# Accumulator banks handed out by the planner, and a planner that tries more orders

## The chip, the core and the metric

The kernel runs on one core of a Trainium2 chip. The core has five engines that run side by side, each through a list of instructions in a fixed order: TensorE (PE in the profile, with its weight loads shown as PEld), VectorE (DVE), ScalarE (ACT), GpSimd (POOL) and SyncE (SP), which issues most DMA transfers. TensorE writes its products into PSUM, eight banks of 128 x 512 numbers, and VectorE or ScalarE reads them from there. The metric is the device time of one execution in microseconds (us); lower is better.

## What is computed

Two layers of a decoder trunk, for 528 positions (16 learned ones and 512 of the input) of width 1024:

```python
for l in range(DEPTH):                       # 2 layers
    xn = rmsnorm(h, norm_mix_g[l])
    z_ret, z_hgrn, z_rwkv, z_s5 = split_cols(xn @ w_in[l], ...)   # 3360 columns
    o_ret  = retention_mixer(z_ret, pos)     # chunkwise retention
    o_hgrn = hgrn2_mixer(z_hgrn, ...)        # gated linear recurrence
    o_rwkv, v_first = rwkv7_mixer(z_rwkv, v_first, ...)   # generalised delta rule
    o_s5   = s5_mixer(z_s5, ...)             # diagonal complex recurrence
    h = h + concat([o_ret, o_hgrn, o_rwkv, o_s5]) @ w_out[l]
    hn = rmsnorm(h, norm_ffn_g[l])
    h = h + square(relu(hn @ w_ffn_up[l])) @ w_ffn_down[l]
return rmsnorm(h, norm_f_g)[:, N_META:]
```

The four mixers of a layer are independent of each other. They need the projections `xn @ w_in`, and the output projection needs all four.

## The kernel before

**Work.** Activations lie with the features across the partitions and the positions along the free dimension. A large product is done in three passes, since each operand is split into a high and a low part: high times high, high times low, low times high. So one tile of a large product is 24 matmuls (8 blocks of 128 input features, three passes) into one bank. Their outputs are called `pi` (input projection), `po` (output projection), `pu` and `pd` (the two halves of the MLP); the number behind `pi_` or `po_` counts weights and so tells how far the layer is. In layer 0 and in both input projections a matmul has 272 or 256 columns; in the rest of layer 1 it has 512. These four kinds are called weight products below. In all there are 7872 of them: 1296 for each input projection, and the first of the second layer stands behind 4752 others.

**Mixers.** Each mixer works through its positions in three segments, named c0, c3, c6 for RWKV (`L0c0` is layer 0, first segment) and c0, c1, c2 for HGRN (`h`) and retention (`r`: `r1c2` is retention in layer 1, last segment). S5 works in two halves. They are chains of small products: a product into a bank, an operation on VectorE or ScalarE that reads it, the next product. In RWKV the products `G..` open a segment's main part, `pak`, `px` to `pt` solve a triangular system, `S`, `zp` and `po00` to `po12` advance the state and make the output, and `pg0`, `pg1` are the last products of a segment. In retention `rs00` to `rs13` are the eight score products of a segment, each read by one VectorE operation that writes `ATr`; `bkr` is the last product of a segment.

**Order.** Nothing is issued as it is written. `Sched.record` collects the operations. `Sched.flush` plans them, three times in the program: up to the middle of the first layer's MLP, from there to the middle of the second layer's, and the rest. `Sched.run` goes through the operations by list scheduling, with a cost for each operation (`price`) and a latency between engines (`lat`): each engine takes, of the operations that are ready, the one with the lowest key. The key is how late an operation may start, taken from a backward run. `attempt` repeats forward and backward runs (ten times, `TURNS`), and the shortest plan is issued, engine by engine in the planned order. Matmuls with another tile shape (such as 64 x 64) are put off for a while to avoid changing the shape (`KEEP`, `SWITCH`).

**Banks.** Before the change `NPS=[3,3,1,1]` splits the eight banks: three for the weight products (`hv`), three for RWKV (`rw`), one for HGRN (`hg`), and one (`mx`) for retention, S5 and the sums of the norms. Within its share, a product uses the banks in turn, in the order in which the program is written, and must wait until the product that had the bank before is read.

**Fill.** While TensorE would be idle, `run` counts fill matmuls on zeros (operand `zero`, line L236) for that gap. `keep_warm` then puts them into a bank of the weight products that is about to be opened, and leaves them out where there is none.

The change is in `Sched` (`tile`, `run`, `flush`, `keep_warm`) and in `ps`, which the mixers call for a bank. All instructions have line L233, since a helper issues them, so they are told apart by their tiles.

Of the kernel before, what the change touches and what calls it, by code (L numbers as in the profile page):

```python
# [49 lines left out]
STEP=1; WARM=6500.0; LEAST=3500.0; SWITCH=.1; DRAIN=.05; KEEP=3.0; WCOLS=256; WCOST=.112; WSAFE=.4; FLB=2; NPRE=3; TURNS=10; NPS=[3,3,1,1]  # L50
# [8 lines left out]
class _Op:  # L59
    __slots__=("e","op","f","a","k","deps","pre","cost","succ","ready","cols","nbytes","chain","label","pri","order","mode","at")  # L60

TICK=10.24/3
# [25 lines left out]
class Sched:  # L88


    def __init__(s,tc):
        s.tc=tc; nc=s.nc=tc.nc
        s.clk={n:.57 for n in ("tensor","vector","scalar","gpsimd","sync")}; s.queue=(.57,0.0); s.recent=[]; s.tiling=(None,None); s.bank={}; s.tag={}; s.idle=None
# [5 lines left out]
    def tile(s,pool,pn,shape,dt,name,tag,bufs,psum=False):  # L99
        x=pool.tile(shape,dt,name=name,tag=tag,bufs=bufs)  # L100
        n=x.tensor.name
        if psum: s.psum.add(n); s.bank[n]=x; s.tag[n]=tag
        s.tags.setdefault((pn,tag),(bufs,[]))[1].append(n)
        return x
# [30 lines left out]
    def run(s,key,back=False):  # L135
# [3 lines left out]
        clk={e:0.0 for e in s.clk} if back else dict(s.clk); hw,dma=(0.0,0.0) if back else s.queue; mode,place=s.tiling; recent=collections.deque(s.recent); act=sum(x for _,x in recent); idle=[0]*N  # L139
        ready={e:[] for e in clk}; late={e:[] for e in clk}  # L140
        left=[len(o.succ if back else o.pre) for o in ops]; at=[0.0 if back else o.ready for o in ops]; T=[0.0]*N; Z=[0.0]*N
        push=heapq.heappush; pop=heapq.heappop
        for i,o in enumerate(ops):
            if not left[i]: push(late[o.e],(at[i],i))
        for _ in ops:
            t=1e18
            for x in clk:
                p=late[x]; r=ready[x]
                while p and p[0][0]<=clk[x]:
                    i=pop(p)[1]; push(r,(key[i],i))  # L150
                u=clk[x] if r else p[0][0] if p else 1e18
                if u<t: t=u; e=x
            p=late[e]; r=ready[e]
            while p and p[0][0]<=t:
                i=pop(p)[1]; push(r,(key[i],i))
            if e!="tensor" or back: i=pop(r)[1]; o=ops[i]; c=o.cost
            else:


                x=r[0]  # L160
                if ops[x[1]].mode!=mode:
                    y=min((y for y in r if y[0]<x[0]+KEEP and ops[y[1]].mode==mode),default=None)
                    if y is not None: x=y
                o=ops[x[1]]
                if o.at is not None and o.mode==mode and o.at==place:
                    y=min((y for y in r if y[0]<x[0]+KEEP and ops[y[1]].mode==mode and ops[y[1]].at!=place),default=None)
                    if y is not None: x=y
                if x is r[0]: pop(r)
                else: r.remove(x); heapq.heapify(r)
                i=x[1]; o=ops[i]; c=o.cost  # L170

                if o.mode!=mode: c+=SWITCH+(DRAIN if place is not None else 0.0)


                if s.idle is not None:
                    p=clk[e]; n=0; w=WCOLS*max(o.mode[0],64)/128.0; d=WCOST if o.at is None else WCOST/2+.002
                    while n<32:
                        while recent and recent[0][0]<p-TICK: act-=recent.popleft()[1]
                        if p+d<=t:
                            if act<WARM: recent.append((p,w)); act+=w; n+=1  # L180
                            p+=d
                            continue
                        while recent and recent[0][0]<t-TICK: act-=recent.popleft()[1]
                        if act>=LEAST: break
                        recent.append((t,w)); act+=w; n+=1; t+=d; p=t
                    idle[i]=n
# [10 lines left out]
            Z[i]=z  # L197
            for j,l in (o.pre if back else o.succ):
# [3 lines left out]
        return T,Z,(clk,(hw,dma),(mode,place),list(recent),idle)  # L202
    def flush(s,turns=0):
# [4 lines left out]
        for (pn,tag),(bufs,names) in s.tags.items():  # L208
            for q,t in enumerate(names):
# [4 lines left out]
                for i in s.users[t]:  # L214
                    if not ops[i].deps&mine: ops[i].deps|=old; ops[i].ready=max(ops[i].ready,at)
        for o in ops: o.pre=[(j,lat(ops[j],o)) for j in o.deps]+[(j,-1e9) for j in o.order]
# [3 lines left out]
        best=None; key=list(range(len(ops)))  # L220
        def attempt(key,n):
            nonlocal best
            for it in range(n):
                if it: key=chain([-z for z in s.run([-z for z in Z],True)[1]])
                T,Z,state=s.run(key); m=max(Z)
                if best is None or m<max(best[1]): best=T,Z,state
# [3 lines left out]
        T,Z,(s.clk,s.queue,s.tiling,s.recent,idle)=best  # L230
        for t in s.users: s.done[t]=max(Z[i] for i in s.users[t])
        for k,i in s.keep_warm(T,idle):
            if k is None: o=ops[i]; e=o.e; x=o.f(*o.a,**o.k)  # L233
            else:
                K,M,p,q=i; e="tensor"
                x=s.nc.tensor.matmul(s.bank[k][q:q+M,:WCOLS],s.idle[p:p+K,:M],s.idle[p:p+K,:WCOLS],start=True,stop=True)  # L236
            if e in s.prev: s.tc.add_manual_dep(x.ins,s.prev[e].ins.name,mybir.DependencyInfo(mybir.DependencyClass.NoSync,mybir.DependencyReason.DATA),reason="order")
            s.prev[e]=x
        s.start()
    def keep_warm(s,T,idle):  # L240


        ops=s.ops; order=sorted((t,i) for i,t in enumerate(T))
        first={}
        for t,i in order:
            o=ops[i]
            if o.e=="tensor":
                n=(o.k["out"] if "out" in o.k else o.a[0]).tensor.name
                if n not in first: first[n]=t
        bufs,names=next(x for (pn,tag),x in s.tags.items() if tag=="hv" and x[1][0] in s.psum)  # L250
        banks=[]
        for q,n in enumerate(names):
            if n in first: banks.append((first[n],0.0 if q<bufs else s.done.get(names[q-bufs],0.0),n,q%bufs))
        banks.sort()
        out=[]; at=0
        for t,i in order:
            if idle[i]:
                while at<len(banks) and banks[at][0]<t: at+=1
                K,M=[max(x,64) for x in ops[i].mode]; d=WCOST if K==M==128 else WCOST/2+.002; p=t-d*idle[i]
                x=banks[at:at+bufs]; x=x[:1] if K==128 else [y for y in x if y[3]==0][:1]+[y for y in x if y[3]==1][:1]  # L260
                if K==64 and len(x)<2: x=[]
                for j in range(idle[i]):
                    if x:
                        _,f,n,_=x[j%len(x)]
                        if f+WSAFE<=p: out.append((n,(K,M,K*(j%len(x)),M*(j//len(x)%(128//M)))))
                    p+=d
            out.append((None,i))
        return out
# [3 lines left out]
def lat(p,c):  # L272
    if p.nbytes: return .92
    if p.e=="tensor" and c.e=="tensor": return 0.0
    return AFTER[p.e]+(.104 if p.e==c.e=="vector" else .092 if p.e==c.e=="scalar" else WAIT[c.e])
def price(o,out,ins,n):
# [882 lines left out]
def build(tc,A,o_ap):  # L1159
# [4 lines left out]
    with tc.tile_pool(name="kp",bufs=1) as kp, tc.tile_pool(name="ps",bufs=1,space=bass.MemoryType.PSUM) as pp:  # L1164
        np_=[0]; nps=dict(zip(("hv","rw","hg","mx"),NPS))
        def ps(shape,nm,tag):
            t=nc.tile(pp,'ps',[128,512],F32,nm,tag,nps[tag],True)
# [439 lines left out]
```

## Time and profile before

| | |
|---|---|
| median of 3 runs | 1575.28 us (1572.36 to 1577.1) |
| the profiled execution: its time | 1566.77 us |
| the profiled execution: span from the first to the last instruction | 1565.0 us |
| mean granted TensorE clock | 0.969 of full speed |
| TensorE busy | 1510.2 us (96%), of it 75.61 us with fill |
| VectorE busy | 928.6 us (59%) |
| ScalarE busy | 585.2 us (37%) |
| GpSimd busy | 422.3 us (30472 instructions on all engines together) |

An execution's time is 1.8 us above its span. A busy TensorE isn't a useful one: fill counts as busy, and a matmul's time in the profile reaches from its start to its end, so that several overlap. How many weight products start in a stretch says more than the busy share.

### The profile page before, as it was taken

The page shows a single profiled execution, that of the slowest core. Times are in us where ns is not written, and L with a number is a line of the kernel's source. Part 1 is how long each engine was busy: PE and PEld are TensorE (multiplying, and loading weights), DVE is VectorE, ACT ScalarE, POOL GpSimd, SP SyncE. Part 2 cuts the span into 40 slices and gives each one's busy share as a digit, 9 for nine tenths or more (in the row PEclk, how much of TensorE's full clock was granted, in tenths as well). Part 3 has the DMA queues.
Part 4 walks back from the last instruction along what each step waited for, and adds up shares of the span by engine and source line. Part 5 has one row for each costly group of instructions (what it writes and reads, how often), then busy time and mean ns, then how long its engine had stood idle before and what let it go on. Part 6 is the DMA issues. An engine that isn't in the chain of part 4 may idle for free.

```text
span 1565.0 us, 30472 instructions
## 1 busy us (share of the span) xinstructions
PE 1510.2 (96%) x11645; PEld 1362.3 (87%) x11645; DVE 928.6 (59%) x2237; ACT 585.2 (37%) x1163; POOL 422.3 (27%) x577
## 2 busy tenths in 40 slices
PE   8999998989999999999999999989999999999997
PEld 7998887778999999999999998876778888888887
DVE  8855897867843337433565357978757333333345
ACT  4334443522442433424433235445225424233342
POOL 3411572413233225332000012232210222222210
PEclk9999999879999999999999999999889999999998
DMA  5545143421323224332346553352302233332332
GB/s 177 168 130 155 55 125 107 113 72 32 95 87 96 90 77 148 102 96 88 118 150 219 156 156 98 106 154 70 95 28 94 95 95 96 96 98 95 95 103 79
DMA packets 143298, 168.54 MB, mean 108 GB/s; under 512 B 52144, under 2 KB 77168, under 8 KB 143152
## 3 DMA queue, kind: packets, MB, share of 16 engines
q1 hardware_dynamic: 143152, 166.59, 35.1%
q8 instruction: 92, 1.51, 0.4%
q14 instruction: 54, 0.44, 0.1%
HBM read 138.65 MB, written 27.56 MB: 106 GB/s over the span
## 4 chain that ended last, share of the span: by engine, by line
PE 83%; DVE 8%; DMA 2%; issue 2%; SPq 2%; POOL 1%; ACT 1%; DVEq 0%; POOLq 0%; ACTq 0%
PE pu L233 23%; PE pd L233 23%; PE pi L233 17%; PE po L233 6%; SPq L233 2%; PE po L236 1%; DVE Irs L233 1%; DMA Em_L1c<-sd 1%; PE s5y2s L233 0%; DMA X_L0c<-sa 0%; PE s5y0s L233 0%; PE pi L236 0%; DVE Jis L233 0%; PE s5g L233 0%; DVE hA L233 0%
## 5 line engine op out<-in xcount | busy, mean ns | idle before, releaser
L233 ACT ACTIVATE wh<-wr 128x512 fp32r<-128x512 f32 (+1 forms) x388 | 243.8, 629 | 537.2 <-PE pd L233 216.2
L233 DVE TENSOR_TENSOR wl<-wr,wh 128x512 fp32r<-128x512 f32 (+1 forms) x388 | 269.6, 695 | 292.5 <-ACT wh L233 287.4
L233 PE MATMUL pi<-xha,wh 128*128 128x256 f32 (+2 forms) x864 | 252.3, 293 | 5.1 <-ACT zs L233 4.1
L233 PE MATMUL pi<-xla,wh 128*128 128x256 f32 (+2 forms) x864 | 250.3, 290 | 1.0 <-DVE xla L233 1.0
L233 PE MATMUL pi<-xha,wl 128*128 128x256 f32 (+2 forms) x864 | 249.8, 290 | 0.0
L233 PE MATMUL pu<-xhf,wh 128*128 128x272 f32 (+2 forms) x768 | 247.0, 322 | 0.0
L233 PE MATMUL pu<-xhf,wl 128*128 128x272 f32 (+2 forms) x768 | 246.7, 321 | 0.0
L233 PE MATMUL pu<-xlf,wh 128*128 128x272 f32 (+2 forms) x768 | 245.5, 320 | 0.0
L233 PE MATMUL pd<-xhh,wh 128*128 128x256 f32 (+2 forms) x736 | 234.6, 319 | 0.0
L233 PE MATMUL pd<-xhh,wl 128*128 128x256 f32 (+2 forms) x736 | 234.1, 318 | 0.0
L233 PE MATMUL pd<-xlh,wh 128*128 128x256 f32 (+2 forms) x736 | 233.0, 317 | 0.0
L233 POOL TENSOR_TENSOR xlh<-fs,xhh 128x272 fp32r<-128x272 f32 (+1 forms) x96 | 92.2, 961 | 298.6 <-DVE fs L233 230.4
L233 PEld LDWEIGHTS pi<-xha,wh 128*128 128x128 f32 (+1 forms) x864 | 161.8, 188 | 9.1 <-ACT zs L233 4.3
L233 PEld LDWEIGHTS pi<-xla,wh 128*128 128x128 f32 (+1 forms) x864 | 162.1, 188 | 3.7 <-DVE xla L233 1.6
L233 PEld LDWEIGHTS pi<-xha,wl 128*128 128x128 f32 (+1 forms) x864 | 162.1, 188 | 1.7 <-issue 0.5
L233 PEld LDWEIGHTS pu<-xlf,wh 128*128 128x128 f32 x768 | 144.6, 188 | 11.3
L233 PEld LDWEIGHTS pu<-xhf,wl 128*128 128x128 f32 x768 | 144.5, 188 | 11.2
L233 PEld LDWEIGHTS pu<-xhf,wh 128*128 128x128 f32 x768 | 144.4, 188 | 10.6
L233 PEld LDWEIGHTS pd<-xlh,wh 128*128 128x128 f32 x736 | 138.5, 188 | 10.0
L233 PEld LDWEIGHTS pd<-xhh,wl 128*128 128x128 f32 x736 | 138.5, 188 | 9.9
L233 PEld LDWEIGHTS pd<-xhh,wh 128*128 128x128 f32 x736 | 138.6, 188 | 9.4
L233 POOL TENSOR_TENSOR h<-h,fd 128x272 f32<-128x272 f32 (+1 forms) x72 | 87.7, 1218 | 183.2 <-DVE fd L233 181.1
(923 smaller groups left out, 2593.1 us busy)
## 6 DMA issues: line engine op xcount, KB each, us to landing
wr<-in_wup SPq DMA_DIRECT2D x128, 256.0 KB
wr<-in_wdn SPq DMA_DIRECT2D x128, 256.0 KB
wr<-in_win SPq DMA_DIRECT2D x104, 256.0 KB
wr<-in_wout SPq DMA_DIRECT2D x32, 256.0 KB
h<-in_x SPq DMA_DIRECT2D x16, 264.0 KB
hD<-h SPq DMA_DIRECT2D x8, 264.0 KB
h<-hD SPq DMA_DIRECT2D x8, 264.0 KB
out<-out SPq DMA_DIRECT2D x8, 256.0 KB
```

The lines of the kernel that those rows point to most:

```text
L233: if k is None: o=ops[i]; e=o.e; x=o.f(*o.a,**o.k)
L236: x=s.nc.tensor.matmul(s.bank[k][q:q+M,:WCOLS],s.idle[p:p+K,:M],s.idle[p:p+K,:WCOLS],start=True,stop=True)
```

## The change

Banks are no longer split. `ps` now asks `Sched.bank` for a name, not for a bank. `CLASS` puts all four users into one class `a`. While `run` plans, a product's first matmul (`opens`) may start only when a bank is free (`can`). It then takes the bank that came free first. Three banks are set aside for the product that is next in the order of the program (`OWN`, `queue_`, `line`); the other five go to whichever product is most urgent. The bank is free again when its last reader in the plan has ended. Fill is planned at the same place, in banks that are free by then, and `keep_warm` is gone. After the ten turns, `flush` makes 30 more tries (`SHAKES`): each starts from the best keys so far, adds a random number with a spread of 1.0 to each, runs three rounds, and keeps the result when the plan is shorter.

```diff
-STEP=1; ...; TURNS=10; NPS=[3,3,1,1]
+STEP=1; ...; TURNS=10; SHAKES=30; SHAKE=1.0; BANKS=8; CLASS=dict(hv='a',rw='a',hg='a',mx='a'); OWN=dict(a=3)
...
+    def bank(s,pool,name,tag):
+        s.pool=pool; n=f"{name}_v{len(s.psum)}"; s.psum.add(n); s.tag[n]=tag
+        return bass.AP(bass.PSumTensorHandle(name=n,shape=[128,512],dtype=F32),0,[[512,128],[1,512]])
...
+        def can(i,t):
+            v=ops[i].opens
+            if v is None: return True
+            if not free or free[0][0]>t: return False
+            c=s.tag[v]; q=s.queue_[c]
+            while line[c]<len(q) and q[line[c]] in place_: line[c]+=1
+            if q[line[c]]==v and own[c]<OWN[c]: return True
+            return extra<spare
...
+                r_=[y for y in r if can(y[1],t)]
+                if not r_: look=t; continue
...
-                x=r[0]
+                x=min(r_)
...
+                if o.opens is not None:
+                    x=min((y for y in free if y[0]<=t and not (o.mode[0]<128 and y[1] in dirty)),default=None) or free[0]
+                    free.remove(x); heapq.heapify(free); v=o.opens; b=x[1]; k=s.tag[v]
+                    if s.queue_[k][line[k]]==v and own[k]<OWN[k]: own[k]+=1
+                    else: extra+=1; k=None
+                    place_[v]=(b,k)
...
+                for v in o.banks:
+                    use[v]-=1; b,k=place_[v]
+                    s.until[v]=max(s.until.get(v,0.0) if use[v]+1<s.count[v] else 0.0,z+(lat(o,PE_) if e!="tensor" else 0.0))
+                    if not use[v]: push(due,(s.until[v],b,k))
...
+            rnd=random.Random(1)
+            for _ in range(SHAKES):
+                m=max(best[1]); key=[x+rnd.gauss(0.0,SHAKE) for x in keys[0]]; attempt(chain(key),3)
...
-    def keep_warm(s,T,idle):
...
-            t=nc.tile(pp,'ps',[128,512],F32,nm,tag,nps[tag],True)
+            t=nc.bank(pp,nm,CLASS[tag])
```

The instructions themselves stay the same but for fill: 1818 mixer and norm matmuls and 7872 weight products in both programs, with 411 fill matmuls before and 462 now. What moves is their order.

On TensorE, in the first layer, this is where RWKV's first segment opens its main part (`G00L0c`), between input projections `pi`. Before:

```order
L233 MATMUL pi_28_128_272_277<-xha_84,wh_263 128x256
L233 MATMUL pi_28_128_272_277<-xla_85,wh_263 128x256
L233 MATMUL pi_28_128_272_277<-xha_84,wl_264 128x256
L233 MATMUL pi_28_128_272_277<-xha_86,wh_263 128x256
L233 MATMUL pi_28_128_272_277<-xla_87,wh_263 128x256
L233 MATMUL G00L0c_468<-rav_L0c_463,bk_L0c_464 128x128 x2
L233 MATMUL G10L0c_469<-rav_L0c_463,bk_L0c_464 128x128
```

And now, with `b` ahead of a bank's name and `v` behind it:

```order
L304 MATMUL bpi_20_128_0_v_2155<-xha_82,wh_206 128x272
L304 MATMUL bpi_20_128_0_v_2155<-xla_83,wh_206 128x272
L304 MATMUL bpi_20_128_0_v_2155<-xha_82,wl_207 128x272
L304 MATMUL bG00L0c_v_2165<-rav_L0c_398,bk_L0c_399 128x128 x2
L304 MATMUL bG10L0c_v_2170<-rav_L0c_398,bk_L0c_399 128x128
```

It stood in projection 28 and stands in projection 20. Counted through the program, 697 of the layer's 1296 input-projection matmuls stand ahead of it before, and 486 now. For the third segment these are 1296 and 988. In the second layer the first segment moves from 937 to 499, the third from 1296 to 960. HGRN and retention go the other way: HGRN's first product of the first layer (`lv1h0c0`) stood behind 936 and now stands behind 1200.

On TensorE, in the second layer, these are retention's score products of the second segment. Before, with products of HGRN (`lv64`, `tmkh`) and RWKV (`tp`) and a weight product between them:

```order
L233 MATMUL rs01r1c_9332<-rqz1c_9323,rkz1c_9325 128x128
L233 MATMUL lv64h1c_9246<-hB_9184,Kh1c_9233 64x128 x3
L233 MATMUL rs11r1c_9333<-rqz1c_9323,rkz1c_9325 128x128
L233 MATMUL rs02r1c_9334<-rqz1c_9323,rkz1c_9325 128x128
L233 MATMUL po_6_2_16_9396<-xho_9305,wh_8907 128x512
L233 MATMUL rs12r1c_9335<-rqz1c_9323,rkz1c_9325 128x128
L233 MATMUL tp01L1c_9131<-cst,rav_L1c_9109 128x128 x3
L233 MATMUL tp11L1c_9132<-cst,rav_L1c_9109 128x128 x3
L233 MATMUL rs03r1c_9336<-rqz1c_9323,rkz1c_9325 128x128
L233 MATMUL tmkh1c_9248<-cst,Kh1c_9233 128x128
```

And now:

```order
L304 MATMUL brs00r1c_v_15128<-rqz1c_9078,rkz1c_9080 128x128
L304 MATMUL brs11r1c_v_15131<-rqz1c_9078,rkz1c_9080 128x128
L304 MATMUL brs02r1c_v_15133<-rqz1c_9078,rkz1c_9080 128x128
L304 MATMUL bzp2L1c_v_15093<-tav_L1c_8959,tbk_L1c_8960 64x64 x3
L304 MATMUL brs12r1c_v_15140<-rqz1c_9078,rkz1c_9080 128x128
L304 MATMUL brs03r1c_v_15143<-rqz1c_9078,rkz1c_9080 128x128
```

The score products stood one by one among others and now nearly follow each other.

On TensorE, in the first layer, this is the end of the mixers, among output projections `po`. Before, the last mixer product is RWKV's `pg1`:

```order
L233 MATMUL po_0_2_272_1008<-xho_758,wh_1001 128x256
L233 MATMUL po_0_2_272_1008<-xlo_759,wh_1001 128x256
L233 MATMUL pg1L0c_700<-g10c_695,sw_141 128x192
L233 MATMUL po_0_2_272_1008<-xho_758,wl_1002 128x256
L233 MATMUL po_0_2_272_1008<-xho_761,wh_1001 128x256
```

Now it is retention's `bkr`:

```order
L304 MATMUL bpo_0_1_0_v_5716<-xho_657,wh_702 128x272
L304 MATMUL bbkr0c_v_5722<-cst,nxr0c_684 128x128 x4
L304 MATMUL bpo_0_1_0_v_5716<-xlo_658,wh_702 128x272
L304 MATMUL bpo_0_1_0_v_5716<-xho_657,wl_703 128x272
L304 MATMUL bpo_0_1_0_v_5716<-xho_559,wh_705 128x272
```

Counted through the program, 1448 weight products stand ahead of the last mixer product before, and 1408 now; in the second layer 6132 before (`pg1L1c`) and 6096 now (`bkr1c`). TensorE changes its tile shape 471 times before and 394 times now.

## Rows read from the trace of the kernel before

**Rows 1.** The page: the span, and busy time of each engine.

```profile
span 1565.0 us, 30472 instructions
PE 1510.2 (96%) x11645; PEld 1362.3 (87%) x11645; DVE 928.6 (59%) x2237; ACT 585.2 (37%) x1163; POOL 422.3 (27%) x577
```

**Rows 2.** Busy time by stretches: length, engines with instruction counts, clock, DMA share, GB/s.

```profile
450.00:500.00 50.00, 50.00 (x412) 50.00 (x411) 20.02 (x35) 16.52 (x32) 15.23 (x18) 1.00 0.28 90
...
1250.00:1300.00 50.00, 50.00 (x218) 40.62 (x217) 17.85 (x27) 13.72 (x23) 13.80 (x9) 1.00 0.31 97
```

**Rows 3.** The same view, for the fill on line L236 alone, all stretches together.

```profile
sum 1565.00, PE 75.61 PEld 36.60; mean PE 2.36 PEld 1.14
```

**Rows 4.** The same view, of all instructions, for the mixers of both layers.

```profile
50.00:150.00 100.00, 98.47 (x832) 94.86 (x830) 63.42 (x198) 36.85 (x77) 28.71 (x68) 0.99 0.49 146
150.00:250.00 100.00, 94.98 (x1075) 83.69 (x1075) 89.78 (x250) 41.61 (x100) 58.95 (x107) 1.00 0.35 99
250.00:390.00 140.00, 127.73 (x1135) 108.29 (x1134) 102.03 (x264) 51.24 (x113) 42.93 (x46) 0.87 0.30 81
...
850.00:950.00 100.00, 100.00 (x816) 96.40 (x815) 53.39 (x114) 34.40 (x69) 8.00 (x13) 1.00 0.53 157
950.00:1050.00 100.00, 90.20 (x1037) 78.17 (x1036) 80.56 (x191) 44.64 (x108) 27.71 (x39) 0.97 0.43 120
1050.00:1171.00 121.00, 113.53 (x913) 87.40 (x912) 89.23 (x221) 42.66 (x91) 28.86 (x27) 0.86 0.24 67
```

**Rows 5.** The chain that ended last, layer 0: start us, length us, what.

```profile
290.94 0.55 PE G10L0c L233
...
324.23 0.74 PE rs00r0c L233 x2
...
358.40 0.48 PE rs00r0c L233 x2
...
389.95 0.52 PE pg1L0c L233 x2
```

**Rows 6.** The same chain, layer 1.

```profile
1076.62 0.86 PE G11L1c L233 x6
```

**Rows 7.** TensorE in order of time, layer 1: start us, length us.

```profile
1170.20 0.59 PE L233 MATMUL pg1L1c<-g11c,sw 32*128 32x192 f32 x2
```

**Rows 8.** Tile ATr1c: VectorE idle before its instructions (us, times), by what ended it.

```profile
  PE rs11r1c L233: 2.6, 2
  PE rs12r1c L233: 1.8, 2
  PE rs13r1c L233: 1.5, 2
  PE rs02r1c L233: 1.2, 2
  PE rs03r1c L233: 1.2, 2
  PE rs10r1c L233: 1.0, 2
  PE rs01r1c L233: 0.4, 1
  PE rs00r1c L233: 0.2, 1
```

**Rows 9.** TensorE in order of time, around a change of tile shape.

```profile
160.84 0.29 PE L233 MATMUL pi<-xha,wl 128*128 128x272 f32 x1
160.97 0.29 PE L233 MATMUL pi<-xha,wh 128*128 128x272 f32 x1
161.19 0.39 PE L233 MATMUL zp0L0c<-tav_L0c,tbk_L0c 128*64 128x64 f32 x6
```

**Rows 10.** Busy time by stretches again, two of 10 us, for the clock.

```profile
320.00:330.00 10.00, 6.96 (x24) 5.51 (x24) 7.55 (x22) 1.43 (x3) 0.42 (x1) 0.57 0.05 17
...
350.00:360.00 10.00, 9.70 (x143) 8.18 (x143) 6.59 (x12) 3.42 (x8) 5.29 (x4) 1.00 0.20 54
```

More of the change, by code (lines that the diff above doesn't have):

```diff
@@ L59 @@
 class _Op:
-    __slots__=("e","op","f","a","k","deps","pre","cost","succ","ready","cols","nbytes","chain","label","pri","order","mode","at")
+    __slots__=("e","op","f","a","k","deps","pre","cost","succ","ready","cols","nbytes","chain","label","pri","order","mode","at","opens","banks")
 TICK=10.24/3
@@ L92, in __init__ @@
         s.tc=tc; nc=s.nc=tc.nc
-        s.clk={n:.57 for n in ("tensor","vector","scalar","gpsimd","sync")}; s.queue=(.57,0.0); s.recent=[]; s.tiling=(None,None); s.bank={}; s.tag={}; s.idle=None
+        s.clk={n:.57 for n in ("tensor","vector","scalar","gpsimd","sync")}; s.queue=(.57,0.0); s.recent=[]; s.tiling=(None,None); s.tag={}; s.idle=None; s.banks=[(0.0,b) for b in range(BANKS)]; s.now=[None]*BANKS
         s.prev={}; s.tags={}; s.psum=set(); s.done={}; s.label=''; s.pri=None; s.after=set()
@@ L142, in run @@
         push=heapq.heappush; pop=heapq.heappop
+        free=sorted(s.banks); due=[]; use=dict(s.count) if not back else {}; place_={}; spare=BANKS-sum(OWN.values()); own=dict.fromkeys(OWN,0); extra=0
+        line={c:0 for c in OWN}; dirty={}
+        def can(i,t):
[6 more added lines that the diff above has]
+            return extra<spare
         for i,o in enumerate(ops):
             if not left[i]: push(late[o.e],(at[i],i))
-        for _ in ops:
+        todo=N; look=0.0
+        while todo:
             t=1e18
@@ L175, in run @@
-                if s.idle is not None:
[L176 to L186, printed above, removed]
+                if o.mode!=mode: c+=SWITCH+(DRAIN if place is not None else 0.0); dirty={}
@@ L201, in run @@
                 if not left[j]: push(late[ops[j].e],(at[j],j))
-        return T,Z,(clk,(hw,dma),(mode,place),list(recent),idle)
+        return T,Z,(clk,(hw,dma),(mode,place),list(recent),sorted(free+[x[:2] for x in due]),idle,place_)
     def flush(s,turns=0):
@@ L229, in flush @@
             best=None; attempt(chain([-z for z in s.run([-z for z in s.run(key)[1]],True)[1]]),turns)
-        T,Z,(s.clk,s.queue,s.tiling,s.recent,idle)=best
+            rnd=random.Random(1)
+            for _ in range(SHAKES):
+                m=max(best[1]); key=[x+rnd.gauss(0.0,SHAKE) for x in keys[0]]; attempt(chain(key),3)
+        T,Z,(s.clk,s.queue,s.tiling,s.recent,s.banks,idle,where)=best
         for t in s.users: s.done[t]=max(Z[i] for i in s.users[t])
[L232 to L236, printed above, removed]
+        real={}
@@ L238, in flush @@
             s.prev[e]=x
-        s.start()
-    def keep_warm(s,T,idle):
[L243 to L268, printed above, removed]
@@ L270 @@
+        for t,i in sorted((t,i) for i,t in enumerate(T)):
+            o=ops[i]
+            for b,K,M,p,q in idle[i] or ():
+                if not hasattr(s.now[b],"tensor"): s.now[b]=s.pool.tile([128,512],F32,name=f"z{b}",tag=f"b{b}",bufs=1)
+                issue("tensor",s.nc.tensor.matmul(s.now[b][q:q+M,:WCOLS],s.idle[p:p+K,:M],s.idle[p:p+K,:WCOLS],start=True,stop=True))
+            issue(o.e,o.f(*[ap(x) for x in o.a],**{k:ap(x) for k,x in o.k.items()}))
+        s.start()
 AFTER={"vector":.07,"scalar":.05,"tensor":.165,"gpsimd":.0}
```

69 lines of the change are left out of this document (55 added, 14 removed).

## The prediction

> **What bounds the kernel now.** I read the page first. TensorE is busy for 1510.2 of 1565.0 us [rows 1], which would leave almost nothing to win. But 75.6 us of that is fill [rows 3], and matmuls overlap in the record, so I counted starts instead. Where weight products run undisturbed, 412 start in 50 us (0.121 us each) with 272 or 256 columns, and 218 start in 50 us (0.229 us each) with 512 columns [rows 2]. No order makes those stretches shorter. Then I read the stretches of the mixers [rows 4]. They have three parts in each layer. First, input projections with little beside them: VectorE is busy 63.4 of 100 us in layer 0 and 53.4 of 100 in layer 1. Then a part in which VectorE is close to full: 89.8 and 80.6 of 100. Then a tail in which there are few weight products left: 102.0 of 140 us and 89.2 of 121, at a mean granted clock of 0.87 and 0.86. So what a schedule can win lies in VectorE's idle time: 36.6 + 46.6 = 83.2 us in the first parts, 38.0 + 31.8 = 69.8 us in the tails.
>
> The chain that ended last says what a tail hangs on. In layer 0 the third RWKV segment opens its main part at 290.94 us, behind all input projections, and its last product starts at 389.95 [rows 5]: 99 us. In layer 1 the same goes from 1076.62 to 1170.20 [rows 6, 7]: 94 us. RWKV's last segment is the tail, and the other mixers run beside it.
>
> **Term 1, one bank for retention's scores.** Before, the eight score products of a segment share the bank `mx` and each waits until VectorE has read the one before. In layer 1 VectorE sat idle for 2.6 + 1.8 + 1.5 + 1.2 + 1.2 + 1.0 + 0.4 + 0.2 = 9.9 us until one of them ended [rows 8]. Now several banks are open and they stand nearly in a row, so the reads can follow each other. The gain is between 0 (VectorE then waits for the next thing) and 9.9 in layer 1, and something like it in layer 0, where more of VectorE's other work lay between. I take 10 for both layers together: the whole of layer 1's, with layer 0's unknown part against what doesn't come back. -10 us.
>
> **Term 2, RWKV begins earlier.** Its first segment opens 211 weight products earlier in layer 0 and 438 earlier in layer 1, and its third segment 308 and 336 earlier. At 0.121 us that is 37 and 41 us for the third segment, 78 us in all, if the projections kept their times and RWKV its speed. They will not: HGRN is put behind instead (its first product of layer 0 behind 264 more weight products), the VectorE work in a layer stays the same, and it now has to pass before the end in a tail that holds HGRN and retention. What is late next is HGRN's and retention's last segment; retention's `bkr` is now the last mixer product in both layers. So the gain isn't the 78 us but what VectorE's idle time in the tails gives up, and that is filled by work only as far as the chains have several products to offer at a time. Of the 69.8 us, 9.9 are in term 1. That leaves 60 as the upper end; the lower end is 0, if the chains of HGRN and retention wait for the same hops between engines as RWKV's did. I take 25, four tenths, nearer to nothing because a segment's steps depend on each other and no bank changes that. -25 us.
>
> **Term 3, changes of tile shape.** There are 77 fewer (471 to 394). One costs about 0.09 us: two equal matmuls start 0.13 us apart (160.84 and 160.97), and with a change behind it the next starts after 0.22 (161.19) [rows 9]. That is 7 us of TensorE time, of which half may lie where TensorE isn't waited for. Ends: 0 and -7. I take -4 us.
>
> **Term 4, weight products that lose their cover.** Before, output projections filled TensorE's gaps while RWKV ended: 1448 weight products stood ahead of the last mixer product in layer 0, and 1408 do now. So 40 more run after it, at 0.121 us, or 5 us. In layer 1 it is 6132 and 6096, 36 at 0.229, or 8 us. These are covered by nothing: behind them the norm and the MLP wait. This term is the surest of the sum, and it is a loss: the mixers must end 13 us earlier before anything is won. +13 us.
>
> **Fill** goes from 411 to 462 matmuls. It stands in TensorE's gaps, beside the waits for VectorE. I take 0; if all 51 lay on the path, at 0.18 us (75.6 us over 411), it would cost 9. The vector, scalar and GpSimd instructions and the transfers are the same ones, so they cost nothing more. The MLP and the third planning round move little; I take 0 there.
>
> **Sum** against the profiled execution's own time: 1566.8 - 10 - 25 - 4 + 13 = 1540.8 us. That execution was 0.5% below the median of the runs shown, 1575.3, so for a median I take 1540.8 x 1575.3 / 1566.8 = 1549 us. Faster or slower by 0.3% of the median, 4.7 us, is about what a measurement can tell.
>
> **Rivals.**
>
> *The tails close further* (deeper gain). With eight banks in one pool, HGRN, retention and RWKV can all have products open, and most of the 60 us goes: 45 instead of 25. Then 1520.8, or 1529 as a median. For it speaks that VectorE reached 89.8 of 100 us where several mixers ran beside projections [rows 4]; against it, that the projections are then gone and each chain alone has waits.
>
> *The clock takes it back.* Now fewer weight products lie in the tails, and those kept the clock up. A pair of score products took 0.74 us at 324 us and 0.48 at 358 [rows 5], with a granted clock of 0.57 and 1.00 there [rows 10]; full speed is 2.4 GHz, and its lower level is 1.2. The time at half clock is now 2 x 0.13 x 140 + 2 x 0.14 x 121 = 70 us in the tails [rows 4]. If all 261 us of both tails were at half clock, 191 us more would run some 35% slower (0.26 of 0.74); with three tenths of that on the path this costs 20 us: 1560.8, or 1569. The Trainium skill, "TensorE: Matmul & The Clock Gate", section "A second HAM failure mode: psum-queue depth-cycling", tells of a kernel that cycled through its banks and whose clock swung between its two levels, because TensorE paused between groups. By that rule this change would look like this rival. The tails before, with a bank or three for each mixer and no pool, already show pauses and both levels, so the trace can't yet tell whether a pool makes it worse; fill in free banks speaks against it.
>
> *Late readers hold the pool* (slower). TensorE's list is in a fixed order. Before, a late reader of HGRN's bank held up HGRN's next product and what stood behind it. Now a bank's next user is whichever product the plan puts there, often of another mixer or a weight product, and the plan's times decide it. If a reader on VectorE is later than planned, the matmul that wants the bank stands at the head of TensorE's list, and all behind it wait: weight products, and the small products for which VectorE and ScalarE wait. A wait for a score product was 9.9 us over 14 times, 0.71 us [rows 8]. There are 436 mixer and norm tiles in the program, besides those of weight products. When 37 of them (one in twelve) are late by that much on the path, the 26 us are gone; when 65 are (one in seven), it loses 20 us: 1586.8, or 1595. The Trainium skill, "PSUM — Partial Sum Buffer", section "Engine vs sequencer instructions", says that matmuls start and complete in program order. It would make such a wait one for all that stands behind, and no row here shows a matmul that went past another. Against this rival: the bank that came free first is taken, so with eight there is some slack, and the wait for a bank was worse with one bank than it can be with five to share.
>
> *It does nothing.* The lists differ on every engine, but the new places of HGRN and retention could cost in the tails what RWKV wins ahead of them; then terms 1 to 3 give 13 and term 4 takes it, near 1575.
>
> **Chances.** Forecast 0.57 (own range 1533 to 1567), deeper gain 0.14, clock 0.09, nothing 0.07, late readers 0.13. Only the first two and the better half of the clock case are faster by over 0.3% (under 1570.6): 0.76. Within it: the other half of the clock case, most of the "nothing", and a little of the late readers: 0.11. Slower: 0.13. The range leaves out the deepest gains and the worse half of late readers: 1518 to 1585.
>
> **What would show it.** Term 1: VectorE's idle time until `rs` products in layer 1 falls from 9.9 to under 3 us. Term 2: the third RWKV segment opens while projections run, `pg1` of the third segment is no longer the last mixer product, and VectorE's busy share in the tails rises from 73% to over 80%; the first weight product of the MLP comes earlier by some 10 us in layer 0 and as much again in layer 1. Term 3 shows as nothing by itself. Term 4: after the last mixer product, output projections run alone for 5 and 8 us longer than before. The stretches of the MLP stay as they were. The forecast is wrong if the clock's mean in the tails falls well under 0.8, or if TensorE shows waits for VectorE or ScalarE at the first matmul of weight products.

## The result, and the profile after

The changed kernel took 1514.57 us (median of 4 runs, 1513.31 to 1518.5), the kernel before beside it 1573.82 (4 runs, 1565.91 to 1577.1). The ratio is 0.9635, with an interval of 0.9594 to 0.9676: about 57 us less, where 26 were forecast. The direction was right. The time lies 3.4 us below the range.

The page of the changed kernel, span and busy times, to be read against [rows 1]:

```profile
span 1511.5 us, 30536 instructions
PE 1468.0 (97%) x11696; PEld 1334.1 (88%) x11696; DVE 922.2 (61%) x2237; ACT 582.1 (39%) x1163; POOL 428.2 (28%) x577
```

The span is 53.5 us shorter. TensorE in order of time says where (start us, length us; a `b` ahead of the name of a product and a `v` behind it are new, the products are the same):

```profile
197.30 0.82 PE L304 MATMUL bG00L0c_v<-rav_L0c,bk_L0c 64*128 64x128 f32 x5
...
332.30 0.48 PE L304 MATMUL bpg0L0c_v<-g10c,sw 32*128 32x192 f32 x2
...
354.31 0.60 PE L304 MATMUL bbkr0c_v<-cst,nxr0c 128*128 128x128 f32 x4
...
387.93 0.29 PE L304 MATMUL bpu_v<-xhf,wh 128*128 128x272 f32 x1
...
768.06 0.37 PE L304 MATMUL bpi_v<-xha,wh 128*128 128x272 f32 x1
...
1076.13 0.48 PE L304 MATMUL bpg1L1c_v<-g11c,sw 32*128 32x192 f32 x2
...
1107.81 0.60 PE L304 MATMUL bbkh1c_v<-cst,nxh1c 128*128 128x128 f32 x4
...
1142.58 0.39 PE L304 MATMUL bpu_v<-xhf,wh 128*128 128x512 f32 x1
```

And the same view of the kernel before, for the third RWKV segment of layer 0, the first products `pu` of each layer's MLP and the first input projection of layer 1:

```profile
289.94 0.49 PE L233 MATMUL G00L0c<-rav_L0c,bk_L0c 64*128 64x128 f32 x2 [1.41 <-DVE bk_L0c L233]
...
420.40 0.29 PE L233 MATMUL pu<-xhf,wh 128*128 128x272 f32 x1
...
799.99 0.37 PE L233 MATMUL pi<-xha,wh 128*128 128x272 f32 x1
...
1195.90 0.39 PE L233 MATMUL pu<-xhf,wh 128*128 128x512 f32 x1
```

Up to the first MLP product the first layer is 420.40 - 387.93 = 32.5 us shorter. Its MLP is not (379.6 us before, 380.1 now). From the first projection of layer 1 to its first MLP product it is 395.9 - 374.5 = 21.4 us less, and the rest is equal again (369.1 and 368.9). So all of it lies ahead of the MLPs, where the mixers are. The third RWKV segment opens at 197.30 us where it opened at 289.94 (290.94 in [rows 5] is where the chain passes it), and its last products are no longer the end: that is retention's `bkr0c` at 354.31 (before: `pg1L0c` at 389.95) and HGRN's `bkh1c` at 1107.81 (before: `pg1L1c` at 1170.20 [rows 7]).

The stretches of the mixers, the view of [rows 4], with the tails cut where the mixers end now:

```profile
50.00:150.00 100.00, 96.34 (x975) 89.56 (x976) 76.87 (x240) 40.11 (x86) 32.20 (x58) 0.98 0.42 121
150.00:250.00 100.00, 94.35 (x973) 87.45 (x973) 85.16 (x242) 34.39 (x81) 59.46 (x109) 0.98 0.44 124
250.00:355.00 105.00, 98.74 (x1027) 84.87 (x1026) 86.90 (x215) 52.50 (x121) 38.92 (x49) 1.00 0.36 101
818.00:918.00 100.00, 97.55 (x958) 87.47 (x957) 70.25 (x180) 37.74 (x82) 11.84 (x17) 0.98 0.46 135
918.00:1018.00 100.00, 93.14 (x933) 85.45 (x932) 74.42 (x174) 38.60 (x91) 24.25 (x26) 0.98 0.45 127
1018.00:1108.00 90.00, 82.21 (x839) 67.90 (x838) 71.72 (x166) 42.28 (x90) 29.80 (x32) 1.00 0.35 104
```

The reader is to take VectorE's busy time (the third number with a count) from the length, part by part, here and in [rows 4]. Its idle time goes from 36.6 to 23.1 and from 46.6 to 29.8 us in the first parts of the two layers: 30.3 less. In the middle parts it grows, from 10.2 to 14.8 and from 19.4 to 25.6: 10.8 more. In the tails it goes from 38.0 to 18.1 and from 31.8 to 18.3: 33.4 less. Its work in these stretches also shrinks by 13.1 us (255.2 to 248.9, and 223.2 to 216.4). Of that, 6.4 us is gone from the whole execution (928.6 to 922.2 us for the same 2237 instructions), and the rest lies outside these stretches now. Together 30.3 - 10.8 + 33.4 + 13.1 = 66.0 us. That is by how much the stretches are shorter (340 to 305 and 321 to 290 us), since they were cut where the mixers end: 35.6 us sooner in layer 0 and 30.5 in layer 1, counted from the layer's first projection. In the first parts it is RWKV that fills the idle time: in the time line of VectorE, its operations take 19.5 and 17.8 us there before and 44.6 and 47.1 now.

VectorE's idle time before the operations `ATr1c`, the view of [rows 8]:

```profile
  PE brs00r1c_v L304: 0.8, 1
  PE brs11r1c_v L304: 0.3, 1
  PE brs10r1c_v L304: 0.2, 1
```

That is 1.3 us, where it was 9.9. The fill on line L303, all stretches together, to be read against [rows 3]:

```profile
sum 1511.50, PE 69.12 PEld 38.20; mean PE 69.12 PEld 38.20
```

There are 51 more fill matmuls, yet they take 6.5 us less in all.

### The profile page after: what moved, and what is told of

It reads as the page before. It is cut to its first block, busy times and chain, and to the rows that moved or that the text cites. A ratio compares the mean times of both kernels' runs of the same rounds, so it can differ in the third digit from the quotient of the medians.

```text
span 1511.5 us, 30536 instructions
## 1 busy us (share of the span) xinstructions
PE 1468.0 (97%) x11696; PEld 1334.1 (88%) x11696; DVE 922.2 (61%) x2237; ACT 582.1 (39%) x1163; POOL 428.2 (28%) x577
## 4 chain that ended last, share of the span: by engine, by line
PE 75%; DVE 11%; DMA 5%; issue 4%; ACT 2%; SPq 1%; POOL 1%; POOLq 0%; DVEq 0%; ACTq 0%
PE bpd_v L304 24%; PE bpu_v L304 23%; PE bpi_v L304 10%; PE bpo_v L304 6%; PE z L303 2%; DVE wl L304 1%; SPq L304 1%; DMA wr<-in_win 1%; POOL t2s L304 1%; DMA sa<-Gm_L1c 0%; DVE Irs L304 0%; DMA vfv01c<-zdv 0%; PE bpor0c_v L304 0%; DMA csr1c<-in_cs 0%; DVE tms L304 0%
## 5 line engine op out<-in xcount | busy, mean ns | idle before, releaser
L304 PE MATMUL bpi_v<-xha,wh 128*128 128x272 f32 (+2 forms) x864 | 253.8, 295 | 1.1 <-DVE ht_L1c L304 0.9
L304 PE MATMUL bpi_v<-xha,wl 128*128 128x272 f32 (+2 forms) x864 | 248.8, 289 | 3.2 <-DVE wl L304 3.2
L304 PE MATMUL bpi_v<-xla,wh 128*128 128x272 f32 (+2 forms) x864 | 247.2, 287 | 0.0
L304 PE MATMUL bpu_v<-xhf,wl 128*128 128x272 f32 (+2 forms) x768 | 246.7, 321 | 0.5 <-DVE wl L304 0.5
L304 PE MATMUL bpu_v<-xhf,wh 128*128 128x272 f32 (+2 forms) x768 | 247.0, 322 | 0.0
L304 PE MATMUL bpu_v<-xlf,wh 128*128 128x272 f32 (+2 forms) x768 | 245.4, 320 | 0.0
L304 PE MATMUL bpd_v<-xhh,wh 128*128 128x256 f32 (+2 forms) x736 | 233.8, 318 | 0.0
L304 PE MATMUL bpd_v<-xhh,wl 128*128 128x272 f32 (+2 forms) x736 | 233.6, 318 | 0.0
L304 PE MATMUL bpd_v<-xlh,wh 128*128 128x256 f32 (+2 forms) x736 | 232.5, 317 | 0.0
L304 PEld LDWEIGHTS bpi_v<-xha,wh 128*128 128x128 f32 (+1 forms) x864 | 161.3, 187 | 5.7 <-DVE ht_L1c L304 1.2
```

The lines of the kernel that those rows point to most:

```text
L304: issue(o.e,o.f(*[ap(x) for x in o.a],**{k:ap(x) for k,x in o.k.items()}))
```

## The experiments

Two theories stood against each other at first. One says that the pool of banks gives the gain, since RWKV's third segment no longer has to wait behind its own share. The other says that the 30 random tries give it, whatever the banks. Every run below is of the changed kernel with the edit shown, unless the text says otherwise. The ratio is to the kernel before on the same chip.

**The pool without the tries.**

```diff
-...; SHAKES=30; ...
+...; SHAKES=0; ...
```

> The changed kernel with the 30 random tries taken out (SHAKES=0): one pool of eight banks, ten turns. The changed kernel took 1514.6 us, the one before 1573.8. Theory A (the pool makes the gain, by letting the mixers' chains run beside each other): 1517 to 1530. Theory B (the search makes it): 1550 to 1575. Theory C (the new fill keeps the clock up, and that makes it): 1517 to 1530 as well, with a clock of 0.985 or more.

1546.08 us, ratio 0.9829 (0.9776 to 0.9882), between the ranges of the theories. So the change without the tries gives about 27 us, and the tries give 1546.1 - 1514.6 = 31.5 more. The 27 us are of the pool together with the new planning of banks and fill; a later run tells these apart. Its third RWKV segment already opens ahead of the end of the projections, and the last mixer product is at 373.60 us (TensorE in order of time):

```profile
212.87 0.37 PE L304 MATMUL bG00L0c_v<-rav_L0c,bk_L0c 64*128 64x128 f32 x1
...
373.60 0.60 PE L304 MATMUL bbkr0c_v<-cst,nxr0c 128*128 128x128 f32 x4
```

Its stretches of layer 0:

```profile
50.00:150.00 100.00, 95.77 (x975) 88.86 (x976) 77.22 (x241) 38.90 (x84) 30.38 (x58) 0.98 0.40 116
150.00:250.00 100.00, 92.95 (x918) 84.37 (x916) 76.72 (x222) 32.50 (x76) 51.12 (x108) 0.90 0.40 109
250.00:374.00 124.00, 114.28 (x1103) 100.71 (x1103) 98.00 (x243) 56.46 (x130) 46.27 (x52) 0.93 0.37 101
```

The first part is as full as with the tries: 22.8 us idle, against 36.6 in the kernel before. But nearly all of that comes back in the middle part, 23.3 us against 10.2. What the tries then add lies behind the first part: the middle part goes from 23.3 to 14.8 us idle, the tail from 26.0 to 18.1.

**The tries without the pool**: the kernel before, with its banks, and 30 tries of the same kind.

```diff
-        best=None; key=list(range(len(ops)))
+        best=None; key=list(range(len(ops))); keys=[key]
...
+            rnd=random.Random(1)
+            for _ in range(SHAKES):
+                key=[x+rnd.gauss(0.0,SHAKE) for x in keys[0]]; attempt(chain(key),3)
```

> The kernel before, with nothing of the change but the 30 random tries after its ten turns. If the search is worth something without the pool: 1545 to 1560. If the old shares leave it nothing (theory A1): 1565 to 1580.

1560.04 us, ratio 0.991 (0.9877 to 0.9944): 14 us. The third segment stays where it was:

```profile
287.43 0.48 PE L236 MATMUL G00L0c<-rav_L0c,bk_L0c 64*128 64x128 f32 x2 [0.49 <-DVE bk_L0c L236]
```

So neither theory holds alone. 27 and 14 us add up to 41 of the 57. The 14 us are one draw of the random numbers.

**Other draws of the tries.** The random numbers of the search were started otherwise, `random.Random(2)` and `random.Random(3)` in place of `random.Random(1)`, and with the first start 90 tries were made.

```diff
-            rnd=random.Random(1)
+            rnd=random.Random(2)
```

> The changed kernel with another seed for the random tries. If the 31 us of the search are its work: 1508 to 1525. If they are one lucky draw: 1530 to 1550.

> The changed kernel with a third seed. No tries gave 1546.1, seed 1 1514.6 and seed 2 1536.6. If seed 1 was a lucky draw: 1525 to 1545. If seed 2 was an unlucky one: 1508 to 1522.

> The changed kernel with 90 random tries instead of 30, the same seed, so its first 30 tries are the same. If tries go on paying: 1490 to 1508. If the plan and the chip part ways at this size: 1508 to 1530.

1536.63 us (0.9764, 0.9734 to 0.9794), 1513.81 us (0.9625, 0.9586 to 0.9664) and 1518.25 us (0.9658, 0.9594 to 0.9721). With the pool the tries gave 9.5, 32.3 and, in the kernel as it is, 31.5 us. So about 22 us of the result depend on the draw. In TensorE's order of time the poor draw loses 13.5 us up to layer 0's first MLP product (401.44 against 387.93) and 4.1 in layer 1's mixers, although its third RWKV segment opens nearly as early (201.76 against 197.30). More tries bring nothing that can be measured.

**The old shares under the new rule**, without and with tries: each user keeps its own banks, opened strictly in the order of the program.

```diff
-...; SHAKES=30; ...; CLASS=dict(hv='a',rw='a',hg='a',mx='a'); OWN=dict(a=3)
+...; SHAKES=0; ...; CLASS=dict(hv='v',rw='w',hg='g',mx='m'); OWN=dict(v=3,w=3,g=1,m=1)
```

> The changed kernel with the old shares of banks (3, 3, 1, 1, each in the order of the program) and no random tries; what stays of the change is that a bank is taken at planning time and that fill is planned into banks that are free then. Theory A: 1560 to 1580, VectorE idle before retention's scores in layer 1 again near 10 us. Theory B: 1565 to 1580. Theory C: 1530 to 1550 with a clock of 0.985 or more, since the fill is the new one.

> The old shares of banks with the 30 random tries. Theory A: 1550 to 1570, the search finding a little within the old shares. Theory B: 1515 to 1530. Theory C: as split_noshake less a little, 1525 to 1545.

1612.04 us (1.0262, 1.0215 to 1.0309) and 1629.0 us (1.0404, 1.0328 to 1.0479). This is not the kernel before in another form: it is 40 us slower than that. The next runs ask why.

**The old rule in the new code**: the same shares, and within a share the banks in turn, as before the change (the edit of the shares above, and the count of a share's open banks that goes with the rule, are left out here).

```diff
-            if q[line[c]]==v and own[c]<OWN[c]: return True
-            return extra<spare
+            i=q.index(v)-OWN[c]
+            return i<0 or (q[i] in place_ and use[q[i]]==0 and s.until[q[i]]<=t)
```

> split_noshake was slower than the kernel before (1612.0 against 1571.7 us). It had the old shares but a new rule: within a share a product could only open after the one ahead of it in the program had opened. This run has the old shares and the old rule (a product of a share of n banks waits until the product n places ahead of it in the program is read), with no random tries; from the change only the planning of banks and fill inside the plan is left. Theory A (the pool and the search make the gain together, the rest of the change does nothing): 1565 to 1580, like the kernel before. Rival D (the new bookkeeping of banks and fill costs time that the pool has to win back): 1590 to 1615.

> As oldrule_noshake, with the 30 random tries. With the pool these were worth 31 us (1546.1 to 1514.6). Theory A1 (the search needs the pool: with old shares the chains leave it nothing to choose): 1560 to 1580. Theory A2 (the search is worth as much by itself): 1535 to 1550.

1611.89 us (1.0234, 1.0197 to 1.027) and, with tries, 1607.66 us (1.0225, 1.0188 to 1.0263). The rule isn't what costs. In the kernel before, the reuse of a bank is a dependence, so the backward run, from which the urgencies come, sees it. The new code plans the banks in the forward run only. The next edit gives the urgencies this back: a product that opens a bank depends on all that use the product which had the bank before.

```diff
+        for c,q in s.queue_.items():
+            for n,v in enumerate(q):
+                if n<OWN[c]: continue
+                mine=set(s.users[v]); old=set(s.users[q[n-OWN[c]]])
+                for i in s.users[v]:
+                    if not ops[i].deps&mine: ops[i].deps|=old
```

> oldrule_noshake took 1611.9 us with the same shares and order rule as the kernel before (1573.8). What it lost with the change are the bank edges in the graph: in the kernel before, a product's operations depend on the readers of the product that had its bank, so the backward run, which makes the urgencies, sees that a bank is scarce; in the changed kernel it doesn't. This run puts these edges back, with no random tries. If blind urgencies cost the 38 us: 1560 to 1582. If it is something else in the new bookkeeping: 1595 to 1615.

> oldrule_deps (1555.1 us: old shares, old rule, bank edges in the graph, new planning of fill) with the 30 random tries. The search was worth 14 us in the kernel before and 9 to 32 us with the pool. If the pool is needed to come near the changed kernel: 1535 to 1555. If the search and the new planning do it without the pool: 1512 to 1530.

1555.11 us (0.9899, 0.9827 to 0.9972), and with tries 1548.51 us (0.9849, 0.9791 to 0.9906). The third RWKV segment opens like this without and with these dependences, one fence for each:

```profile
345.34 1.65 PE L303 MATMUL bG10L0c_v<-rav_L0c,bk_L0c 64*128 64x128 f32 x6
```

```profile
286.03 0.37 PE L309 MATMUL bG00L0c_v<-rav_L0c,bk_L0c 64*128 64x128 f32 x1
```

So urgencies that don't know of fixed shares cost 57 us. With them known, and the old shares and rule, the segment opens about where it did before the change. That the time is then still 18 us under the kernel before is not explained. In the profiled executions most of it lies in layer 1's mixers, with a higher clock there. The rows go from the layer's first projection to the end of its last mixer product, in the view of [rows 4], the kernel before and then this run:

```profile
799.99:1170.47 370.48, 351.79 (x3166) 309.74 (x3165) 251.21 (x610) 139.09 (x297) 70.15 (x102) 0.94 0.42 122
```

```profile
797.70:1158.21 360.51, 351.39 (x3288) 310.74 (x3287) 248.08 (x610) 138.61 (x297) 68.64 (x102) 0.99 0.44 126
```

This run is the one to measure the pool against, since both have the new planning of banks and fill. Against its 1555.1 us the pool gives 9 us and the tries alone 6.6; the intervals overlap, so neither is clear of noise. Both together give 40.5 us. With tries on both sides, the pool gives 1548.5 - 1514.6 = 34 us in the first draw, 35 in the third and 12 in the second, each clear of noise; the old shares had one draw only.

Why the pool gives so little without the tries shows in the same view. With the old shares, layer 0 up to the end of its last mixer product (layer 1 is the row above), and then with the pool, both layers:

```profile
0.00:388.54 388.54, 365.76 (x3465) 328.86 (x3466) 295.63 (x867) 151.35 (x328) 147.24 (x261) 0.96 0.41 114
```

```profile
0.00:373.92 373.92, 348.81 (x3354) 317.52 (x3355) 292.60 (x861) 149.52 (x325) 144.25 (x260) 0.95 0.41 118
787.00:1140.80 353.80, 338.07 (x3172) 303.99 (x3171) 244.35 (x603) 135.98 (x293) 73.56 (x100) 0.95 0.44 127
```

The third RWKV segment opens 73 us earlier in layer 0, yet the mixers end only 14.6 us sooner there and 6.7 in layer 1. And from there to the first MLP product it takes 33.7 and 33.2 us with the pool, 28.9 and 25.4 with the old shares: 12.5 us of the 21.3 are lost again. This is the loss of term 4 of the prediction: weight products that run behind the last mixer product.

**One user held back at a time.** HGRN keeps one bank, RWKV three, or retention, S5 and the norms one; the others share the rest, three of it in the order of the program as before; no tries. In the first three runs the urgencies know nothing of it; in the last two they do, by the dependences above for that user alone, which then also takes its banks in turn.

```diff
-            return extra<spare
+            return c=='a' and extra<spare
```

> pool_noshake (1546.1 us) with one thing taken back: retention, S5 and the sums of the norms share one bank again, in order; the other users have the pool of seven. Term 1 of the prediction put 10 us on retention's scores. If one bank for these users is where the pool gains: 1556 to 1575, VectorE idle before retention's scores in layer 1 near 10 us again. If the gain comes from RWKV and HGRN: 1540 to 1555.

> pool_noshake (1546.1 us) with HGRN alone held to one bank, in order. Taking the pool from retention, S5 and the norms cost 12.8 us. If the gain of the pool is spread over its users: 1552 to 1565. If retention and S5 had most of it: 1540 to 1552.

> pool_noshake (1546.1 us) with RWKV alone held to three banks, in order. The prediction saw RWKV's last segment as the tail of each layer. If RWKV needs more than three banks, or another order of them, for the gain: 1560 to 1590. If three banks are enough for it: 1538 to 1552.

> pool_hg1_noshake (1579.8 us) held HGRN to one bank and also left the planner blind to that bank when it makes the urgencies. This run holds HGRN to one bank with the edges of that bank in the graph, as the kernel before has them. If HGRN's one bank is what the pool removes: 1562 to 1585. If the loss was the blind urgencies: 1540 to 1558.

> The same for RWKV: three banks in the old rotation, with the edges in the graph; pool_rw3_noshake without them took 1590.7 us, pool_noshake 1546.1. If three banks in rotation hold RWKV back: 1560 to 1590. If the loss was the blind urgencies: 1540 to 1558.

| held back | urgencies | us | ratio | above the pool's 1546.1 |
|---|---|---|---|---|
| retention, S5, norms | blind | 1558.84 | 0.9903 (0.9867 to 0.9939) | 12.8 |
| HGRN | blind | 1579.76 | 1.0067 (1.0032 to 1.0102) | 33.7 |
| RWKV | blind | 1590.71 | 1.0132 (1.007 to 1.0193) | 44.6 |
| HGRN | informed | 1563.12 | 0.9934 (0.9908 to 0.996) | 17.0 |
| RWKV | informed | 1582.98 | 1.0108 (1.0046 to 1.0171) | 36.9 |

RWKV in three banks costs most. Its third segment then opens late again (first row, informed). But it also opens late when only HGRN is held (second row, informed):

```profile
285.15 0.68 PE L313 MATMUL bG00L0c_v<-rav_L0c,bk_L0c 64*128 64x128 f32 x4 [0.42 <-DVE bk_L0c L313]
```

```profile
278.78 0.35 PE L313 MATMUL bG00L0c_v<-rav_L0c,bk_L0c 64*128 64x128 f32 x1 [1.33 <-DVE rav_L0c L313]
```

So a late start isn't the work of RWKV's own share alone. In both rows, and in the kernel before, what released the product was an operand from VectorE, not a bank. Where the banks held up the work ahead of it was not shown. The RWKV runs have another open end: they leave the other users five banks, three of them in the order of the program, so only two go to whichever product is most urgent, where the pool has five. What RWKV's three banks cost and what this narrower choice costs the others wasn't tested apart.

The costs don't add: 12.8 + 17.0 + 36.9 is 66.7 us, more than the 27 that the pool gives. RWKV held alone, at 1583.0 us, is even slower than all users held (1572 in the kernel before, 1555.1 in the new code). For the first run, VectorE's idle time before `ATr1c` until a score product ended was this:

```profile
  PE brs12r1c_v L304: 0.7, 2
  PE brs13r1c_v L304: 0.5, 1
  PE brs03r1c_v L304: 0.3, 1
  PE brs11r1c_v L304: 0.2, 1
  PE brs01r1c_v L304: 0.2, 1
```

That is 1.9 us, not 9.9, although the scores have their one bank back. So that bank costs 12.8 us by the medians (the intervals just touch, and the urgencies are blind), but not in the wait that the prediction showed.

**Fill and clock.** In one run the plan is made without fill. In the other it is made with it, and the fill matmuls are not issued. Both leave out fill alone, which no output uses.

```diff
-                        while len(fill)<32:
+                        while False:
```

```diff
-            for b,K,M,p,q in idle[i] or ():
+            for b,K,M,p,q in ():
```

> The changed kernel with no fill at all while planning (also none at the start); pool and random tries stay. Theory A: 1515 to 1530, a lower clock that costs a few us. Theory B: the same. Theory C: 1545 to 1575 with a mean clock of 0.96 or less and 80 us or more at half clock.

> The changed kernel with the same plan and order, but the 462 fill matmuls are not issued. pool_nofill had no fill and another plan and took 1514.8 us at a clock of 0.971. If the clock that fill holds up is worth nothing on the path: 1508 to 1520 with a clock near 0.95. If it is worth something, and pool_nofill's plan made up for it: 1525 to 1545.

1514.81 us (0.9648, 0.9599 to 0.9697) and 1518.11 us (0.9645, 0.9615 to 0.9675). The intervals hold the 0.9635 with fill. The mean clock of the second:

```profile
core 0: 1518.8 us, clock 0.968
```

## Why the prediction was right in direction and too small

**Term 2 is the step that failed.** It took its size from VectorE's idle time in the tails alone. It said: "So the gain isn't the 78 us but what VectorE's idle time in the tails gives up." The tails gave about what terms 1 and 2 ask of them together, 33.4 us of idle time for a forecast of 35. But an RWKV that begins earlier also fills VectorE's idle time where the projections run. The first parts gave 30.3 us, and the middle parts took back 10.8. Another 13.1 us of VectorE's busy time left the mixers' stretches. The prediction had read the 83.2 us of idle time in the first parts, said that a schedule can win there, and then gave them no term. These parts make 30.3 - 10.8 + 13.1 = 32.6 us. With them the forecast of 26 would have been 58.6, and the span fell by 53.5. Term 2's 25 should have been about 52, if terms 1 and 3 stand as forecast: 66.1 us by which the mixers end sooner, less 10 and 4.

**The tries had no term of their own.** The positions were read from the order as issued, so what the search did was in them, but it wasn't sized. The change without the tries is worth 27 us, by chance what was forecast for everything: without them the first part of layer 0 gains 13.8 us of VectorE's idle time and the middle part loses 13.1. The tries add 31.5 us in this draw. With the pool they gave 32, 31.5 and 9.5 us, with the old shares 14 and 6.6, one draw each. That a search wins more where the pool leaves it room fits two of three draws, and isn't shown beyond them.

**Term 1** was near in size (12.8 us when the bank is taken back, 10 forecast), though that run holds S5 and the norms to the bank too. Its sign in the profile came true, 9.9 us down to 1.3, but the run with one bank shows that the price isn't paid there. Where it is paid stays open, so the near size may be luck.

**Term 3** was not tried alone.

**Term 4** was right. From the last mixer product to the first MLP product, layer 0 goes from 420.40 - 389.95 = 30.5 us to 387.93 - 354.31 = 33.6, and layer 1 from 25.7 to 34.8: 12.2 us more, for 13 forecast. Divided by layers it was off (5 and 8 forecast, 3.2 and 9.1 measured). The reading that retention's `bkr` is the last mixer product in both layers holds in layer 0; in layer 1 it is HGRN's `bkh1c`, with the same number of weight products ahead of it.

**Fill** at nothing holds: without it the time is the same within the intervals.

**Two readings to set right**, on which no term rests. RWKV's third segments begin at 289.94 and 1073.71 us and so take 100 and 97 us, not 99 and 94. And in the clock rival, a pair that goes from 0.48 to 0.74 us is 54% longer, not 35%; that rival would have cost 31 us, not 20.

**The signs.** VectorE's share in the tails rose from 73% to (86.90 + 71.72) / 195 = 81%. The third segment opens among projections, `pg1` isn't last, and the MLP's stretches are equal. The first MLP product came 32.5 and 21.4 us sooner in its layer, where 10 was named.

**The rivals.** *The tails close further* had the direction, but its 1529 us also came from the tails alone. *The clock takes it back* is false. The clock in the tails rose from 0.87 and 0.86 to 1.00, and the time at half clock, 2 x (1 - clock) x span, fell from 97 to 21 us between the profiled executions. The Trainium skill, "TensorE: Matmul & The Clock Gate", section "A second HAM failure mode: psum-queue depth-cycling", tells of a kernel that cycled through its banks and whose clock swung between its levels. Read as a rule for pools, it would have this kernel lose clock. The trace doesn't agree: 0.993 against 0.969, and 0.968 with the pool and no fill issued. *Late readers hold the pool* is not seen: all weight products together wait 4.8 us, where it was 7.2 before, and for their operands. The group that waits most waits for the low part of its weights (the page of the changed kernel, busy and mean, then idle time and its releaser):

```profile
L304 PE MATMUL bpi_v<-xha,wl 128*128 128x272 f32 (+2 forms) x864 | 248.8, 289 | 3.2 <-DVE wl L304 3.2
```

**What stays open**: why the old shares and rule in the new code are 18 us faster than the kernel before; which user's banks make the pool's gain; why the tries made the split shares slower (1612.0 to 1629.0 us), though a try is kept only when its plan is shorter; and what in a draw decides.

## What to carry to other kernels

When a chain begins earlier, count the idle time of the engine that it needs along the whole way, also where another engine is full, and not only at the end that it leaves. A pool of banks and a search over orders are to be tried together: here the pool gave 9 us without the search, not clear of noise, and 12 to 35 with it. If shares are fixed, the urgencies of a list scheduler must see them, or that costs more than the shares. A random search over orders is worth a term of its own, and one draw tells little of it: here three draws lay 23 us apart.

## What the hardware showed that was not expected

The mean clock and the time came apart. Without the fill matmuls the tails ran at 0.87 and 0.85, much as in the kernel before, where with fill it was 1.00:

```profile
250.00:355.00 105.00, 95.82 (x877) 83.01 (x876) 85.02 (x210) 52.01 (x124) 40.12 (x50) 0.87 0.37 101
...
1018.00:1108.00 90.00, 81.81 (x715) 67.70 (x715) 67.75 (x157) 41.70 (x89) 27.04 (x31) 0.85 0.36 104
```

In the two profiled executions that is 2 x 0.032 x 1518.8 = 97 us at the lower of the two levels without fill, and 21 us with it. By the median clocks of the four executions of each, 0.9695 and 0.989, it is 92 and 33 us. Yet the median times are 1518.1 and 1514.6 us. That is some 59 us more at half clock for 3.5 us between the medians, and by the ends of the intervals for not over (0.9675 - 0.9594) x 1573 = 13 us. If the end waited for TensorE in that time, half of it, 30 us, would have been lost. So TensorE at its lower level was mostly not what the end waited for, unless the fill matmuls themselves cost about what their clock gives back, which these runs don't tell apart.
